# Eight k-tiles instead of six through seven block products in the gate and up projections of a decoder layer

## The chip, the cores and the metric

The kernel runs on one core of a Trainium2 chip. Its time is the device time of one launch in microseconds (us), as the median of three runs. The weights lie in HBM in float32, 461 MB are read from it in a launch, and the token block is short (256 tokens), so every weight is read once and used for two blocks of 128 tokens.

## The reference

One layer: half a SwiGLU, a mixer (dilated attention beside a gated spatial unit, merged by two sigmoid gates), half a SwiGLU again, and a final norm. The change is in the gate and up projections of the two SwiGLUs; the rest moves only because it shares buffers with them.

```python
def swiglu(x, w_gate, w_up, w_down):
    return (jax.nn.silu(x @ w_gate) * (x @ w_up)) @ w_down

x = x + 0.5 * swiglu(rmsnorm(x, ffn1_norm[i]), ffn1_w_gate[i], ffn1_w_up[i], ffn1_w_down[i])
x = x + hybrid_mixer(rmsnorm(x, mix_norm[i]), ...)
x = x + 0.5 * swiglu(rmsnorm(x, ffn2_norm[i]), ffn2_w_gate[i], ffn2_w_up[i], ffn2_w_down[i])
```

x is 256 x 2048, gate and up are 2048 x 5632, down is 5632 x 2048.

## The kernel before

**Products.** A float32 product is made of three TensorE matmuls on operands split in a high and a low part: high by high, high by low, low by high. The weight of a k-tile (128 rows, 512 columns) is split by two instructions: ACT copies it to `wh` (L356), and DVE subtracts `wh` from it to give `wl` (every DVE instruction has line L66, the wrapper that keeps count of DVE's work). `wh` and `wl` are rings of nine k-tiles. One matmul takes 128 tokens' activations as its weights and 512 columns of `wh` or `wl` as its moving operand, and all of them have line L363.

**Steps.** The program is one list of steps. A plain step ("n") is two k-tiles of one column group of 512: one load of 512 KB to a `raw` tile, one split on ACT and one on DVE, and 12 matmuls (two k-tiles, two token blocks, three matmuls). A loop over the steps writes out each step's products, then whatever has come due (evacuations, transpositions), then the splits of the steps ahead for which the ring has room, then additions that are put off until DVE has time. All engines work off what is theirs in that order.

**Seven products.** Two column groups that are computed together (gate and up of the same columns, or two column groups of down) and two token blocks form a 2 x 2 block product over some of the k-tiles, paired two by two. A "quad" does such a pair of k-tiles in seven block products (the Strassen and Winograd scheme) instead of eight, which are 21 matmuls and not 24. For that it needs seven forms of the four weight blocks, `p1` to `p7`: three are the blocks b11, b21 and b22 themselves; f is a sum of two blocks (mostly added by an accumulating DMA from the POOL queue while it is loaded), and t2, t1 and t4 are made by DVE additions. Each form is split like a raw tile and takes a quarter of a plain step per pair of k-tiles. Sums of the activations (`fx`, `fy`, `fh`) are needed too; they are made once. Between forms, partial results in PSUM are copied (ACT, L415, L417, L419) and added (DVE). The forms of a quad begin in the tail of the group before (`p1`, `p6`, `p7`) and end in the first half of its own (`p5`, `p4`, `p3`, `p2`).

**The two SwiGLUs.** There are 11 column groups of gate and up each. The first two of the first SwiGLU and the first of the second are done in other ways; the other 9 and 10 are quads over three pairs (six of the sixteen k-tiles), with ten plain steps for the rest. `silu` of gate is taken by ACT (L614) when gate's sum is complete, the product with up by DVE when up's is, then DVE transposes the result, a DMA writes it to DRAM and four read it back as the left operand of down. The tile `sg` in which this happens has two buffers (tag `tmp`). Loads of raw tiles (five buffers, and seven units more in the tiles C and E at the very start) are issued on the SP queue (L256), blocks of quads too (L298).

Of the kernel before, what the change touches and what calls it, by code (L numbers as in the profile page):

```python
# [44 lines left out]
RAWB = 5  # L45
MORE = 7
# [25 lines left out]
def layer(ctx: ExitStack, tc: tile.TileContext, a, out):  # L72
# [75 lines left out]
    def lay_out():  # L148
        i, count = 0, 0
        while i < len(gemms):  # L150
# [8 lines left out]
            if quad:  # L159
# [4 lines left out]
                quad["todo"] = ["t2", "t1", "t4"] if quad["adds"] else ["f", "t2", "t1", "t4"]  # L164
                for k, form in opening(count):
                    steps.insert(len(steps) - k, ("s", (quad, form)))
                for k, form in reversed(list(closing(len(order)))):
                    new.insert(k, ("s", (quad, form)))
# [8 lines left out]
        for kind, s in steps:  # L177
            width = 2 if kind == "n" else s[0]["nq"]
# [4 lines left out]
            if kind == "s":  # L183
                s[0].setdefault("at", {})[s[1]] = len(ends) - 1
# [56 lines left out]
    raws = {}  # L241

    def load_unit(i, first=0, end=2):
        if i not in raws and RAWB <= i < RAWB + MORE:
# [3 lines left out]
            raws[i] = raws["more"][:, 2 * o:2 * o + 2]  # L250
        if i not in raws:
            raws[i] = big.tile([P, 2, NC], F32, tag="raw", bufs=RAWB, name=f"raw{i}")
# [9 lines left out]
    def ffn_home(home):  # L262
        home["h"] = [big.tile([P, 16, S], F32R, tag=tag, name=f"h{tag}") for tag in "AB"]
        c, e = (big.tile([P, 4096], F32, tag=tag, name="quads") for tag in "CE")
        w = sb.tile([P, SGW], F32, tag="W", name="sum")
        b11, b21, b12, b22, t2 = (v.rearrange("p (q c) -> p q c", q=3)
                                  for v in (c[:, 0:SGW], c[:, SGW:2 * SGW], e[:, 0:SGW], e[:, SGW:2 * SGW], w))
        return b11, b21, b12, b22, t2, b11, e[:, 2 * SGW:2 * SGW + NC]
# [7 lines left out]
    def merge_home(home):  # L276
        l_ = sb.tile([P, 3, 2, NC], F32, tag="L", name="quads")
        w = sb.tile([P, 3, NC], F32, tag="W", name="part")
        t = sb.tile([P, 2, NC], F32, tag="tmp", bufs=2, name="sum")
# [12 lines left out]
    def load_block(quad, b):  # L292
# [6 lines left out]
        if b == 2 and quad["adds"]:  # L299
            POOL.dma_start(blocks_of(quad)[b], block(quad, 3), accum_op=OP.add)  # L300
# [46 lines left out]
    def split(i, k=None):  # L347
        kind, s = steps[i]
        if kind == "s":
            prepare_for(*s)  # L350
            s[0]["split"].add(s[1])
        r = raws[place[i]] if kind == "n" else form_of(*s)
# [5 lines left out]
        if kind == "s" and s[1] in FREES:  # L358
            at(now[0] + (1 if s[1] == "p5" else 2), lambda: load_block(next_of(s[0]), FREES[s[1]]))
# [952 lines left out]
```

## Time and profile before

| what | before |
|---|---|
| median of three runs | 1985.66 us (1984.95 to 1985.70) |
| the profiled execution | 1985.29 us, its span 1983.5 us |
| TensorE (PE) busy | 1971.1 us, 99% of the span, 9188 instructions |
| DVE busy | 1592.2 us, 80%, 1655 instructions |
| ACT busy | 1189.5 us, 60%, 1382 instructions |
| granted TensorE clock | 0.999 |
| DMA | 492.34 MB, mean 248 GB/s |

A row of a group of instructions reads: line, engine, operation, result<-operands, shape, count, then the busy time and the mean of one. In the table by windows each engine has its busy time in the stretch and, in brackets, how many of its instructions touch it; overlapping instructions of one engine count once. In a timeline the first number is the start and the second the duration, both in us. In a list of waits the numbers are the total, the count and the longest.

### The profile page before, as it was taken

What the parts mean: (1) busy time and instruction counts of PE and PEld (TensorE: products, weight loads), DVE (VectorE), ACT (ScalarE), POOL (GpSimd) and SP (SyncE); (2) the same over time, 40 slices, a digit from 0 to 9 for tenths busy, and PEclk for the clock granted to TensorE, in tenths of its full rate; (3) what the DMA queues carried; (4) which work ended last, traced back from release to release, by engine and by line L of the source; (5) the groups of instructions that cost most, each with busy time, mean ns of one, the idle gap of its engine ahead of it and who ended that gap; (6) DMA issues with size and microseconds to landing.
All of it is one profiled execution on the core that took longest, in us unless ns stands there. A gap on an engine that the chain in (4) does not pass through costs nothing.

```text
span 1983.5 us, 25183 instructions
## 1 busy us (share of the span) xinstructions
PE 1971.1 (99%) x9188; PEld 1723.6 (87%) x9188; DVE 1592.2 (80%) x1655; ACT 1189.5 (60%) x1382; POOL 51.7 (3%) x48
## 2 busy tenths in 40 slices
PE   9999999999999999999999999999999999999998
PEld 8888888888888888888888888878888888888887
DVE  6798888888897798766665777888898889888886
ACT  7566556665666676555454555576655566565664
POOL 0000100000000000000000000000000000000000
PEclk9999999999999999999999999999999999999999
DMA  9788778787777985888877667788888777878783
GB/s 323 256 279 271 237 238 266 247 254 245 247 242 226 289 294 186 254 275 255 264 238 249 210 204 231 237 260 267 255 252 260 234 249 247 252 250 254 244 265 123
DMA packets 264644, 492.34 MB, mean 248 GB/s; under 512 B 17484, under 2 KB 46024, under 8 KB 264392
## 3 DMA queue, kind: packets, MB, share of 16 engines
q1 hardware_dynamic: 253624, 469.49, 72.0%
q0 software_dynamic: 10576, 20.71, 6.0%
q8 instruction: 72, 1.18, 0.2%
q10 hardware_dynamic: 320, 0.53, 0.1%
q14 instruction: 52, 0.43, 0.1%
HBM read 461.01 MB, written 29.66 MB: 247 GB/s over the span
## 4 chain that ended last, share of the span: by engine, by line
PE 95%; DVE 2%; DMA 1%; issue 1%; ACT 0%; SPq 0%; POOLq 0%; POOL 0%; DVEq 0%; ACTq 0%
PE qd L363 71%; PE mm L363 22%; DVE wl L66 1%; DMA raw<-in_w_in_dram 0%; DMA quads<-in_w_in_dram 0%; DVE btx L66 0%; ACT wh L356 0%; PE sp L815 0%; PE warm L1180 0%; DMA xt<-bmx 0%; DVE xlo L66 0%; PE pv L990 0%; PE sc L953 0%; DVE x L66 0%; DVE quads L66 0%
## 5 line engine op out<-in xcount | busy, mean ns | idle before, releaser
L66 DVE TENSOR_TENSOR wl<-raw,wh 128x1024 fp32r<-128x1024 f32 (+1 forms) x636 | 695.7, 1112 | 184.5 <-ACT wh L356 182.8
L356 ACT ACTIVATE wh<-raw 128x1024 fp32r<-128x1024 f32 (+1 forms) x636 | 609.1, 966 | 365.8 <-PE qd L363 199.6
L363 PE MATMUL qd<-wh,xlo 128*128 128x512 f32 x1201 | 455.4, 379 | 1.0 <-DVE xlo L66 1.0
L363 PE MATMUL qd<-wh,xhi 128*128 128x512 f32 x1201 | 455.3, 379 | 0.0
L363 PE MATMUL qd<-wl,xhi 128*128 128x512 f32 x1201 | 455.2, 379 | 0.0
L356 ACT ACTIVATE wh<-quads 128x1536 fp32r<-128x1536 f32 (+2 forms) x226 | 250.9, 1117 | 271.1 <-PE qd L363 251.5
L66 DVE TENSOR_TENSOR wl<-quads,wh 128x1536 fp32r<-128x1536 f32 (+2 forms) x226 | 291.0, 1301 | 147.7 <-ACT wh L356 147.5
L363 PEld LDWEIGHTS qd<-wh,xlo 128*128 128x128 f32 x1201 | 227.0, 189 | 33.9 <-DVE xlo L66 1.8
L363 PEld LDWEIGHTS qd<-wh,xhi 128*128 128x128 f32 x1201 | 227.0, 189 | 32.4 <-issue 0.2
L363 PEld LDWEIGHTS qd<-wl,xhi 128*128 128x128 f32 x1201 | 227.0, 189 | 32.2
L363 PE MATMUL mm<-wh,xlo 128*128 128x512 f32 x608 | 230.6, 379 | 0.9 <-DVE xlo L66 0.8
L363 PE MATMUL mm<-wh,xhi 128*128 128x512 f32 x608 | 231.1, 380 | 0.1
L363 PE MATMUL mm<-wl,xhi 128*128 128x512 f32 x608 | 228.5, 379 | 0.0
L363 PE MATMUL qd<-wh,hA 128*128 128x512 f32 x564 | 213.8, 379 | 0.0
L363 PE MATMUL qd<-wl,hA 128*128 128x512 f32 x564 | 213.8, 379 | 0.0
L363 PE MATMUL qd<-wh,hB 128*128 128x512 f32 x564 | 213.8, 379 | 0.0
L356 ACT ACTIVATE wh<-sum 128x1024 fp32r<-128x1024 f32 (+2 forms) x85 | 101.4, 1196 | 86.7 <-PE qd L363 66.9
L66 DVE TENSOR_TENSOR wl<-sum,wh 128x1024 fp32r<-128x1024 f32 (+2 forms) x85 | 117.8, 1395 | 18.0 <-ACT wh L356 16.5
L363 PEld LDWEIGHTS mm<-wh,xlo 128*128 128x128 f32 x608 | 114.9, 189 | 17.8 <-DVE xlo L66 1.6
L363 PEld LDWEIGHTS mm<-wh,xhi 128*128 128x128 f32 x608 | 114.9, 189 | 16.2 <-ACT xhi L547 0.2
L363 PEld LDWEIGHTS mm<-wl,xhi 128*128 128x128 f32 x608 | 114.9, 189 | 16.1
L363 PE MATMUL qd<-wh,fx 128*128 128x512 f32 x352 | 119.2, 379 | 1.0 <-DVE part L66 1.0
(417 smaller groups left out, 2191.2 us busy)
## 6 DMA issues: line engine op xcount, KB each, us to landing
raw<-in_w_in_dram SPq DMA_DIRECT2D x168, 512.0 KB, 4.9
raw<-in_ffn_w_down_dram SPq DMA_DIRECT2D x120, 512.0 KB, 5.0
raw<-in_ffn_w_up_dram SPq DMA_DIRECT2D x112, 512.0 KB, 6.0
raw<-in_ffn_w_gate_dram SPq DMA_DIRECT2D x111, 512.0 KB, 4.2
quads<-in_ffn_w_gate_dram SPq DMA_DIRECT2D x38, 768.0 KB, 6.4
quads<-in_ffn_w_up_dram SPq DMA_DIRECT2D x38, 768.0 KB, 5.1
quads<-in_ffn_w_down_dram SPq DMA_DIRECT2D x32, 512.0 KB, 5.4
quads<-in_ffn_w_up_dram POOLq DMA_DIRECT2D x17, 768.0 KB, 10.6
```

Of the source, the lines that this page charges most:

```text
L66: return method(out, *args, **kwargs)
L356: ACT.activation(wh, r[:, first:end], AF.Copy)
L363: PE.matmul(g["ps"][t], act, in_turn(w), start=not g["begun"][t], stop=g["left"][t] == 0, skip_group_check=g["quad"] is not None)
```

## The change

Quads of gate and up take four pairs (eight k-tiles) instead of three, so such a group has eight plain steps instead of ten. A form of four pairs would take four of the nine slots of the ring at once; it is written as two pieces of two pairs, each with its own ACT and DVE split, and the additions that make it are still one instruction, over 2048 columns instead of 1536. The accumulating DMA of f is issued in two pieces as well.

The larger blocks need room. The tile W, one buffer of `tmp` and one raw tile are given up, and a tile V of 2688 columns takes W's place; t2 and a partial sum of the quads lie in V. With one `tmp` buffer a column group can't begin its `sg` while the one before still uses it, so `silu` moves from gate's end to up's end, and `holds` puts it off by a step as long as the tile is in use. In the mixer a second `tmp` (in V) and a fifth raw tile (`spare`) come back. The sums `fy` are made for two pairs instead of one, since eight k-tiles need them. The four blocks of a first quad are loaded spread over five steps and not at once.

```diff
-RAWB = 5
-MORE = 7
+RAWB = 4
+MORE = 8
...
+                chunks = [(0, nq)] if nq < 4 else [(q, q + 2) for q in range(0, nq, 2)]
                 for k, form in opening(count):
-                    steps.insert(len(steps) - k, ("s", (quad, form)))
+                    for c in chunks:
+                        steps.insert(len(steps) - k, ("s", (quad, form, *c)))
...
+    V = sb.tile([P, SGW + 9 * P], F32, name="V")
+    turns = dict(raw=0, tmp=0, both=False, held=False)
+
+    def five(i):
+        return not turns["held"] and any(hus[i][0]["w"] is w for w in in_mixer)
...
     def move_in(home):
         home["room"] = home["make"](home)
-        for b in (0, 2, 3, 1):
-            load_block(next(q for q in quads if q["home"] is home), b)
+        first = next(q for q in quads if q["home"] is home)
+        for b, wait in ((0, 0), (2, 1.5), (3, 3), (1, 5)):
+            at(now[0] + wait, lambda b=b: load_block(first, b))
...
         if b == 2 and quad["adds"]:
-            POOL.dma_start(blocks_of(quad)[b], block(quad, 3), accum_op=OP.add)
+            for q in range(0, quad["nq"], 2):
+                c = slice(q, min(q + 2, quad["nq"]))
+                POOL.dma_start(blocks_of(quad)[b][:, c], block(quad, 3)[:, c], accum_op=OP.add)
...
             elif n != 1 and c == CS[n] + 1:
-                sums_of(i + lag, xT, 2, 1, forms_tile(big, "k2", f"fy{n}", 1), src, f"y{n}", tag)
+                sums_of(i + lag, xT, 2, 2, store, src, f"y{n}", tag)
...
-                quad = dict(k0=4 * CS[n], nq=2 if late else 3, forms=xT, home=merge if late else home)
+                quad = dict(k0=4 * CS[n], nq=2 if late else 4, forms=xT, home=merge if late else home)
...
+                    if not early:
+                        if holds["sg"]:
+                            at(e + 1, lambda: me["again"](e + 1, banks))
+                            return
+                        me["go"]()
+                    sg = me["sg"]
+                    holds["sg"] = 2 if first == 0 or first == 1 and quads_here["nq"] == 3 else 1
...
-            while loaded < len(hus) and loaded < place[done] + RAWB:
+            while loaded < len(hus) and loaded < place[done] + (5 if five(loaded) else 4):
```

Three places show what moves. The first is DVE's queue in the first SwiGLU, from the splits of `p1` of one quad to the addition that makes t1 (`quads<-sum,quads`, later `quads<-V,quads`); `sum` or V holds t2 there, and `wl<-quads`, `wl<-sum` and `wl<-V` are splits of forms. Before:

```order
L66 TENSOR_TENSOR wl<-quads,wh 128x1536 x2
L66 TENSOR_TENSOR sum<-quads 128x1536
L66 TENSOR_TENSOR wl<-raw_2216,wh 128x1024
L66 TENSOR_TENSOR wl<-raw_2251,wh 128x512 x2
L66 TENSOR_TENSOR wl<-sum,wh 128x1536
L66 TENSOR_TENSOR wl<-raw_2266,wh 128x1024
L66 TENSOR_TENSOR quads<-sum,quads 128x1536
```

And in the changed kernel:

```order
L66 TENSOR_TENSOR wl<-quads,wh 128x1024 x2
L66 TENSOR_TENSOR wl<-quads,wh 128x512 x2
L66 TENSOR_TENSOR wl<-quads,wh 128x1024
L66 TENSOR_TENSOR V<-quads 128x2048
L66 TENSOR_TENSOR wl<-raw_2228,wh 128x1024
L66 TENSOR_TENSOR wl<-raw_2276,wh 128x1024
L66 TENSOR_TENSOR wl<-V,wh 128x1024 x2
L66 TENSOR_TENSOR wl<-raw_2314,wh 128x1024
L66 TENSOR_TENSOR quads<-V,quads 128x2048
```

`p2` of one quad and `p1` of the next stand together in both; they are two instructions of 1536 columns before and four pieces of 1024 now (one of them cut in two where the ring wraps around). The plain steps between the forms are the same here, and the additions are a third longer.

The second is ACT's queue at the same quads: where `silu` (L614, later L655) of one column group stands, with the copy of a partial sum ahead of it (L415 follows `p1`, L450 follows `p7`). Before:

```order
L356 ACTIVATE wh<-sum 128x1536
L356 ACTIVATE wh<-raw_2266 128x1024
L415 ACTIVATE qd_0_2379<-qd_3_2382 128x512
L614 ACTIVATE sg117.5_2371<-qd_0_2105,rstd_440 128x512
L614 ACTIVATE sg117.5_2371<-qd_1_2106,rstd_440 128x512
L356 ACTIVATE wh<-raw_2297 128x1024
```

And in the changed kernel:

```order
L387 ACTIVATE wh<-quads 128x1024 x2
L450 ACTIVATE qd_1_2408<-qd_3_2410 128x512
L655 ACTIVATE sg117.5_2540<-qd_0_2129,rstd_439 128x512
L655 ACTIVATE sg117.5_2540<-qd_1_2130,rstd_439 128x512
L387 ACTIVATE wh<-raw_2417 128x1024
L498 ACTIVATE fh109.5_2443<-fsh109.5_2523 128x4x256
L387 ACTIVATE wh<-V 128x1024 x2
```

The pair of `silu` instructions moves from behind `p1` to behind `p7`, about half a group later, and there are still two.

The third is DVE's queue at the entry to the second SwiGLU, where `xt_1` is the second quarter of the normalized and transposed activations, and `fsy` and `fy` are sums of it and their low parts. Before:

```order
L66 TENSOR_TENSOR fsy_9714<-xt_1_9617 128x128
L66 TENSOR_TENSOR fsy_9714<-xt_1_9617,fsy_9714 128x128
L66 TENSOR_TENSOR wl<-raw_9601,wh 128x1024
L66 TENSOR_TENSOR sum<-quads,sum 128x1024
L66 TENSOR_TENSOR xlo_9402<-xt_1_9617,xhi_9401 128x1024
L66 TENSOR_TENSOR fy_9737<-fsy_9714,fy_9737 128x512
```

And in the changed kernel:

```order
L66 TENSOR_TENSOR fsy_9735<-xt_1_9638 128x256
L66 TENSOR_TENSOR fsy_9735<-xt_1_9638,fsy_9735 128x256
L66 TENSOR_TENSOR wl<-raw_9645,wh 128x1024
L66 TENSOR_TENSOR V<-quads,V 128x1024
L66 TENSOR_TENSOR xlo_9423<-xt_1_9638,xhi_9422 128x1024
L66 TENSOR_TENSOR fy2spare<-fsy_9735,fy2k_9758 128x1024
```

Each of the first two rows stands twice in the queue. The order is the same; the sums and the low part are twice as wide.

More of the change, by code (lines that the diff above doesn't have):

```diff
@@ L249, in load_unit, with tmp @@
                 raws["more"] = big.tile([P, 8, NC], F32, tag="C" if i == RAWB else "E", name=f"more{i}")
-            raws[i] = raws["more"][:, 2 * o:2 * o + 2]
+            return raws["more"][:, 2 * o:2 * o + 2]
+        turns["raw"] = (turns["raw"] + 1) % 5 if five(i) else 0
+        if turns["raw"] == 4:
+            return big.tile([P, 2, NC], F32, tag="spare", name=f"raw{i}")
+        return big.tile([P, 2, NC], F32, tag="raw", bufs=RAWB, name=f"raw{i}")
+    def tmp(shape, name):
+        turns["tmp"] = 1 - turns["tmp"] if turns["both"] else 0
+        if not turns["tmp"]:
+            return sb.tile(shape, F32, tag="tmp", name=name)
+        n = 1
+        for k in shape[1:]:
+            n *= k
+        v = V[:, SGW:SGW + n]
+        names = "abcd"[:len(shape) - 1]
+        return v.rearrange(f"p ({' '.join(names)}) -> p {' '.join(names)}", **dict(zip(names, shape[1:])))
+    def load_unit(i, first=0, end=2):
         if i not in raws:
-            raws[i] = big.tile([P, 2, NC], F32, tag="raw", bufs=RAWB, name=f"raw{i}")
+            raws[i] = raw_room(i)
         g, u, j = hus[i]
@@ L263, in ffn_home @@
         home["h"] = [big.tile([P, 16, S], F32R, tag=tag, name=f"h{tag}") for tag in "AB"]
[L264 to L268, printed above, removed]
+        c, e = (big.tile([P, 2, 4, NC], F32, tag=tag, name="quads") for tag in "CE")
+        t2 = V[:, 0:4 * NC].rearrange("p (q c) -> p q c", q=4)
+        return c[:, 0], c[:, 1], e[:, 0], e[:, 1], t2, c[:, 0], V[:, 4 * NC:5 * NC]
     def gate_home(home):
@@ L422, in read, with sums_of @@
                 DVE.tensor_tensor(q12, x_, part, op=OP.add)
-        after_splits.append(read)
-        if form in ("p1", "p7", "p5"):
-            (second if form == "p5" else first)["begun"][form == "p7"] = True
+        if q1 == quad["nq"]:
+            after_splits.append(read)
+            if form in ("p1", "p7", "p5"):
+                (second if form == "p5" else first)["begun"][form == "p7"] = True
         close(g, i)
-    def sums_of(i, keep, q0, nq, store, v, name, tag="gate", slack=1):
+    def sums_of(i, keep, q0, nq, store, v, name, tag="gate", slack=1, then=None):
         got = {}
@@ L587, in layer @@
     sides = [0]
+    holds = dict(sg=0)
     homes = []
@@ L840, in post @@
         def post(e, banks):
[L841 removed]
+            q = tmp([P, NT, NSLOT, HD], f"{key}{gi}")
             one = 2 * NSLOT * P
```

95 lines of the change are left out of this document (58 added, 37 removed).

## The prediction

> **What bounds the kernel now.** I read the page's head first, then the chain of waits in order of time, PE's own list of waits, and windows laid on single gate and up groups.
>
> ```profile
> span 1983.5 us, 25183 instructions
> PE 1971.1 (99%) x9188; PEld 1723.6 (87%) x9188; DVE 1592.2 (80%) x1655; ACT 1189.5 (60%) x1382; POOL 51.7 (3%) x48
> ...
> DVE  6798888888897798766665777888898889888886
> ```
> ```profile
> 96.55 543.91 PE qd L363 x2520
> ...
> 1327.49 642.74 PE qd L363 x2976
> ```
>
> The two long pieces of the chain are the two SwiGLUs from their first quads on: for 544 and 643 us the chain never leaves PE. A busy PE can still be slow, but here the pieces give its pace: 543.91/2520 and 642.74/2976 are both 0.216 us a matmul, and that is what one costs when it is removed.
>
> PE's waits, from its own list:
>
> ```profile
> PE qd L363 <- DVE part L66: 1.0, 1, 1.0
> PE qd L363 <- DVE xlo L66: 1.0, 2, 0.8
> PE warm L1180 <- PEq L1295: 0.8, 1, 0.8
> PE mm L363 <- DVE xlo L66: 0.8, 1, 0.8
> PE qd L363 <- DVE wl L66: 0.6, 1, 0.6
> ```
>
> They are 4.2 us in all. So PE sets the end, by the number of its matmuls, and a change that removes matmuls is worth their time as long as everything that feeds PE keeps up. The feeder that is nearest to not doing so is DVE. From the table by windows (PE, PEld, DVE, ACT, POOL, clock, DMA), where the first six are gate and up groups of 39.5 us:
>
> ```profile
> 99.00:138.50 39.50, 39.50 (x185) 34.59 (x184) 37.59 (x43) 25.60 (x28) 1.30 (x1) 1.00 0.86 280
> ...
> 257.00:296.50 39.50, 39.50 (x185) 34.59 (x184) 31.46 (x28) 23.63 (x27) 1.29 (x1) 1.00 0.74 231
> 296.50:336.00 39.50, 39.50 (x185) 34.59 (x184) 34.83 (x34) 25.31 (x27) 1.28 (x1) 1.00 0.80 252
> ...
> 1369.80:1409.30 39.50, 39.50 (x185) 34.53 (x184) 33.82 (x32) 25.42 (x27) 1.28 (x1) 1.00 0.79 246
> 1409.30:1448.80 39.50, 39.50 (x185) 34.59 (x185) 35.88 (x35) 24.75 (x26) 0.26 (x1) 1.00 0.83 263
> ...
> 1646.30:1685.80 39.50, 39.50 (x185) 34.59 (x184) 35.69 (x34) 24.79 (x28) 1.22 (x1) 1.00 0.84 259
> ```
> ```profile
> 1305.00:1330.00 25.00, 22.44 (x101) 18.53 (x101) 24.96 (x31) 19.51 (x30) 0.00 (x0) 1.00 0.76 235
> ...
> 745.00:775.00 30.00, 30.00 (x141) 26.27 (x140) 29.71 (x36) 21.97 (x30) 0.00 (x0) 1.00 0.48 150
> ```
>
> A group needs 31.5 to 37.6 us of DVE in 39.5. The last two rows show what a full DVE does: at the entry to the second SwiGLU it is busy for 24.96 of 25 us and PE loses 2.56 us; in the mixer it is busy for 29.71 of 30 us and PE loses nothing. Saturation alone does not decide; what counts is whether the ring's nine k-tiles cover the lateness.
>
> **The matmuls removed.** Nine groups of the first SwiGLU and ten of the second go from three pairs to four, and each pair saves one block product, 3 matmuls: 19 x 3 = 57, at 0.216 us 12.3 us. A group falls from 39.5 us (183 matmuls) to 180 x 0.216 = 38.9 us.
>
> **What DVE gets in return.** Starts that follow each other in DVE's timeline give what an instruction takes from the queue:
>
> ```profile
> 318.68 1.22 DVE L66 TENSOR_TENSOR wl<-raw,wh 128x1024 fp32r<-128x1024 f32 x1
> 319.82 1.75 DVE L66 TENSOR_TENSOR quads<-sum,quads 128x1536 f32<-128x1536 f32 x1
> 321.49 1.22 DVE L66 TENSOR_TENSOR wl<-raw,wh 128x1024 fp32r<-128x1024 f32 x1
> 322.62 0.68 DVE L66 TENSOR_TENSOR wl<-quads,wh 128x512 fp32r<-128x512 f32 x1
> ```
>
> 1.14 us for 1024 columns and 1.67 for 1536, so 0.535 more for each 512, and 2.21 for 2048 (an estimate from these two). Each instruction starts some 0.08 us before the one ahead has ended. Per group: seven forms as two pieces, 7 x (2 x 1.14 - 1.67) = +4.3; two plain steps fewer, -2.3; three additions of 2048 columns and not 1536, +1.6. That is +3.6 us of DVE in a group that is 0.6 us shorter. 34.83 becomes 38.4 of 38.9. Of the 19 groups, ten hold 33.8 to 37.6 us now and stay under 38.9 but for three: 37.59 + 3.6 is over by 2.3, 35.88 by 0.6, 35.69 by 0.4, together 3.3 us. The other nine, of which 257.00 is one, end near 35 and have air. Bounds for what this costs PE: nothing (745 to 775 us, full for 30 us without a stall) and, at the price of the entry, 2.56 us for each of ten groups, 26 us. A bound below nothing has no reason, since no work leaves DVE. I take half of the 3.3, 1.6 us, because the lateness of one group is made up in a lighter one and the ring hides some, while those that go over stay late for many steps.
>
> [...]
>
> **The entry to the second SwiGLU.** PE waits there for DVE's chain, and `fy` is in it.
>
> ```profile
> 1300.90 0.38 DVE L66 TENSOR_TENSOR fsx<-xt 128x256 f32<-128x256 f32 x1
> ...
> 1302.33 1.22 DVE L66 TENSOR_TENSOR wl<-quads,wh 128x1024 fp32r<-128x1024 f32 x1
> ...
> 1319.55 0.28 DVE L66 TENSOR_TENSOR fsy<-xt 128x128 f32<-128x128 f32 x1
> ...
> 1320.47 1.22 DVE L66 TENSOR_TENSOR wl<-raw,wh 128x1024 fp32r<-128x1024 f32 x1
> ...
> 1323.88 0.68 DVE L66 TENSOR_TENSOR fy<-fsy,fy 128x512 fp32r<-128x512 f32 x1
> 1324.48 1.22 DVE L66 TENSOR_TENSOR wl<-quads,wh 128x1024 fp32r<-128x1024 f32 x1
> ...
> 1326.75 0.68 DVE L66 TENSOR_TENSOR part<-part,qd 128x512 f32<-128x512 f32 x1
> ```
>
> Sums of two pairs (`fsx`) take 1.43 us, those of one (`fsy`) 0.92; the low part `fy` takes 0.60 and would take 1.14. That is 1.05 us more ahead of `part`, for which PE waits 1.0 us already, so it comes through whole: between 0 (if another wait covers it) and 1.05, I take 1.05. At the entry to the first SwiGLU the same sums fall into a stretch where DVE is six to seven tenths busy (the first two slices of the page's DVE line).
>
> **What lies beside other work.** ACT has 25 of 39.5 us: the form pieces and `silu` fit. `silu` is two instructions as before; at up's end they stand ahead of one raw split, and gate's banks are next wanted by the quad after the next. `holds` puts off only two column groups, by two steps and one, in the first SwiGLU, where nothing asks for them before down. Between `p6` and `p7` one plain step is left of two, 12 x 0.216 = 2.6 us, and in it ACT must copy PE's result:
>
> ```profile
> L417 ACT ACTIVATE quads<-qd 128x512 f32<-128x512 f32 x31 | 18.0, 579 | 0.0
> ...
> L356 ACT ACTIVATE wh<-raw 128x1024 fp32r<-128x1024 f32 x506 | 531.9, 1054 | 347.1 <-PE qd L363 192.2 <-PE mm L363 119.5 <-DMA raw<-in_w_in_dram 12.0
> ```
>
> One split ahead of it and the copy are 1.63 us. If that cover went, PE would lose up to 1.6 us in each of 19 groups; the step is there in all.
>
> POOL issues two accumulating DMAs of 512 KB for one of 768 KB, and behind them on its queue stands nothing until the next quad. Raw loads have four tiles for five, so a load is issued one plain step later:
>
> ```profile
> raw<-in_ffn_w_up_dram SPq DMA_DIRECT2D x112, 512.0 KB, 6.0
> ...
> quads<-in_ffn_w_up_dram POOLq DMA_DIRECT2D x17, 768.0 KB, 10.6
> quads<-in_ffn_w_down_dram POOLq DMA_DIRECT2D x8, 512.0 KB, 7.9
> ```
>
> Two in sequence are 16 us in a group of 39. For raw tiles: four plain steps without forms are 10.4 us; landing 6.0, ACT 1.05 and DVE 1.2 make 8.3, and in a group with forms the four steps stretch to some 19 us. In the mixer the fifth tile is back.
>
> **The sum.** The profiled execution took 1985.29 us, 0.37 less than the median, and its span lies 1.8 us inside it; neither offset moves, so the sum can stand on the median: 1985.66 - 12.3 + 1.6 + 1.05 = 1976.0 us.
>
> **The rivals.**
>
> 1. The full gain. The ring hides all of DVE's excess and the entry's extra second falls beside another wait: 1985.66 - 12.3 = 1973.4. For it: 745 to 775 us, and only 3.3 us of excess in 750 us. Against it: PE's list has DVE in nearly every line.
>
> 2. Late loads eat most of it. For it: ACT already waits for raw tiles where steps are plain and unbroken.
>
> ```profile
> ACT wh L356 <- DMA raw<-in_w_in_dram: 12.9, 10, 2.2
> ...
> ACT wh L356 <- DMA raw<-in_ffn_w_gate_dram: 6.7, 6, 4.1
> ```
>
> A tile fewer makes a load 2.6 us later. Over the six of the last row that is 15.6 us more of ACT's waiting; the ring has kept all of the 6.7 us from PE so far, and if it keeps two thirds of the new ones too, 5 us are left: 1976.0 + 5 = 1981. Against it: none of these waits reaches PE's list.
>
> 3. DVE becomes the bound. If instructions hide nothing of each other, a group's DVE time is what the durations sum to: 34.83 plus 34 x 0.08 is 37.6; added are 7 x (2.44 - 1.76) - 2.44 + 3 x 0.54 = 3.9; the group takes 41.5 us instead of 39.5. Ten groups lose 2.0, nine still gain 0.6: 1985.66 + 20 - 5.4 = 2000. It decides from the point at which such a group needs over 39.5 us, that is 1.1 us more than my 38.4. Idle time of DVE that can't be used, because the ring is full and DVE waits for ACT and ACT for PE, does the same; it is 4.7 us a group now (39.5 - 34.83), and must fall under 0.5.
>
> That the change doesn't do what it says I give no chance: the matmuls are counted from the loops.
>
> **How the numbers follow.** The forecast 50%, the full gain 27%, late loads 14%, DVE as the bound 9%. A difference of 0.2%, 4 us, is what this kernel's runs can tell from none, so faster is under 1981.7. The forecast and the full gain are faster, late loads are so in half: 84%; the other half of them and a little of the third are the same, 9%; slower 7%. The range reaches from 1972.5, which is the full gain and a microsecond of the entry's old waits, to 1982.5, where late loads end; beyond it lies DVE as the bound.
>
> **What would show it.** Right: 57 fewer matmuls; chain pieces still unbroken in both SwiGLUs at 0.216 us a matmul; windows of 38.9 us on gate and up groups with DVE at 35 to 39 us in them; PE's waits some 7 us, with `part` at the entry near 2. Wrong: waits of PE for `wl` or of ACT for `raw` that repeat once a group (late DVE, late loads), a wait of PE for L448 between `p6` and `p7`, or of ACT's L655 for the one `tmp` tile. The forecast falls if groups last 39.5 us or more.

## The result, and the profile after

The changed kernel takes 2032.39 us (median of four runs, 2025.32 to 2033.30) against 1985.31 us before on the same chip: the ratio is 1.0232, with a 95% interval of 1.0208 to 1.0256. The forecast was 1976.0 us, in a range from 1972.5 to 1982.5: both the sign and the range were missed.

The head of the page and the chain of waits by engine and line, after:

```profile
span 2031.6 us, 25234 instructions
PE 1981.2 (98%) x9131; PEld 1719.4 (85%) x9131; DVE 1660.8 (82%) x1745; ACT 1231.9 (61%) x1472; POOL 76.8 (4%) x69
...
PE 62%; DVE 8%; DMA 6%; issue 5%; ACT 1%; POOL 0%; SPq 0%; DVEq 0%; POOLq 0%; ACTq 0%
PE qd L394 43%; PE mm L394 18%; DVE wl L66 5%; DMA quads<-in_ffn_w_up_dram 3%; DMA raw<-in_w_in_dram 1%; ACT wh L387 1%; DMA quads<-in_w_in_dram 1%; DVE V L66 1%; DMA xt<-bmx 1%; DMA bmh529.0_10447<-bth529.0_10444 0%; DVE quads L66 0%; ACT xt L611 0%; POOL quads L329 0%; DVE xlo L66 0%; DVE btx L66 0%
```

PE has the 57 matmuls fewer (9131 for 9188), and yet it is busy 10 us longer, and the chain now leaves PE for DVE, for DMAs and for time at which nothing is waited for. PE's own list of waits, after:

```profile
PE qd L394 <- DVE wl L66: 27.2, 22, 5.5
PE mm L394 <- DVE wl L66: 7.8, 4, 3.6
```

Before, the first of these rows was 0.6 us in a single wait. PE stands still for `wl` 26 times, for 35 us. The windows (columns as before) show what such waits look like from three sides:

```profile
347.30:389.00 41.70, 39.85 (x181) 33.73 (x180) 39.37 (x39) 30.49 (x36) 2.75 (x3) 1.00 0.80 247
534.70:573.60 38.90, 38.90 (x182) 34.06 (x181) 35.87 (x35) 23.89 (x26) 2.82 (x3) 1.00 0.84 268
...
465.00:475.00 10.00, 4.72 (x22) 3.78 (x20) 3.23 (x2) 2.30 (x3) 0.00 (x0) 0.93 0.66 185
475.00:480.00 5.00, 4.75 (x11) 3.85 (x12) 5.00 (x7) 2.72 (x4) 0.00 (x0) 0.50 0.63 191
```

The second row is a group as forecast: 38.9 us, PE never idle. The first is one that is not: 41.7 us, with DVE idle for 2.3 us of them. The last two rows lie where a down part of the first SwiGLU ends and gate and up of column group 8 begin. There PE stands for half of ten microseconds, and DVE and ACT are idle for two thirds and three quarters of them, so nobody is saturated, somebody waits for data. And after the wait the granted clock is 0.50: PE "busy" for 4.75 us does 11 matmuls. Five stalls are followed by such a stretch, 58 matmuls in all, which take some 13 us more than they would at full pace. Together with some 0.26 us by which the matmuls at the two ends of most stops are longer, they are why PE is busy for longer with fewer matmuls.

To see where the time came from I took, for each quad, the time from its first `p5` matmul to that of the next quad, less 0.216 us for each matmul between, and subtracted the same of before. This gives the loss by place, in us:

| place | changed kernel |
|---|---|
| first SwiGLU's entry (start to the first quad's `p5`) | 7.9 |
| gate and up quads that follow a down quad (three of the four lose: at 470, 1580 and 1805 us) | 21.0 |
| other groups of the two SwiGLUs | 21.0 |
| entry to the mixer (PE stands between 719 and 725 us) | 8.6 |
| entry to the second SwiGLU | 1.3 |
| matmuls removed, 57 x 0.216 | -12.3 |
| sum | 47.5 |

The spans differ by 48.1 us. The gain of the products is there; four late feeds take it away. Each shows in the trace.

**The first SwiGLU's entry.** The timeline of ACT and DVE:

```profile
72.52 1.06 ACT L387 ACTIVATE wh<-raw 128x1024 fp32r<-128x1024 f32 x1 [2.82 <-DMA raw<-in_ffn_w_gate_dram]
80.54 2.28 DVE L66 TENSOR_TENSOR V<-quads 128x2048 f32<-128x2048 f32 x1
83.96 2.32 DVE L66 TENSOR_TENSOR wl<-raw,wh 128x1024 fp32r<-128x1024 f32 x2
```

ACT, and DVE behind it, wait for a raw tile; from then on DVE has no pause, and the splits of the last row, for which PE stands 2.96 us, are behind `t2` of the first quad (the row at 80.54). ACT waits for a raw tile here before the change too, 4.1 us at the longest, and PE does not stand; so the raw tile alone is not the cause.

**The quads behind a down quad.** The timeline at the first of the three that lose, in the first SwiGLU (POOL, then DVE and PE):

```profile
453.64 1.22 POOL L329 DMA_DIRECT2D quads<-in_ffn_w_up_dram  x1 [31.61 <-DVE hB L66]
462.18 1.21 POOL L329 DMA_DIRECT2D quads<-in_ffn_w_up_dram  x1 [7.32 <-issue]
...
471.77 2.29 DVE L66 TENSOR_TENSOR V<-quads 128x2048 f32<-128x2048 f32 x1 [7.04 <-DMA quads<-in_ffn_w_up_dram]
473.98 2.35 DVE L66 TENSOR_TENSOR wl<-raw,wh 128x1024 fp32r<-128x1024 f32 x2
...
475.25 0.79 PE L394 MATMUL qd<-wl,hA 128*128 128x512 f32 x1 [5.53 <-DVE wl L66]
```

POOL issues the first accumulating DMA of 512 KB at 453.64 and the second 8.5 us later, and in between the profile names nothing that it waits for ("issue"; of the 17 such pairs, 6.3 to 10.4 us apart, nine have the name of some DVE instruction there). The landings tell more than these names: in all 17 pairs the second is issued 0.26 to 0.34 us after the first has landed. The two never overlap. `t2` (`V<-quads`) needs the whole accumulated block, DVE takes its queue in order, and so two splits of raw tiles that were ready (ACT had ended their `wh` at 465.42 and 467.36 us) stand behind it for some 7 us and start at 473.98, and PE stands 5.5 us behind them.

**The other groups.** From ACT's list of waits:

```profile
ACT wh L387 <- DVE V L66: 39.3, 18, 6.8
...
ACT sg117.5_2540 L655 <- DVE fsh109.5_2523 L66: 5.2, 1, 5.2
...
ACT sg200.5_4079 L655 <- DVE fsh192.5_4062 L66: 4.8, 1, 4.8
```

There are six waits of the second kind, 29.0 us in all: `silu` wants the one transposition tile, in which DVE has not yet read the last column group's values for the sums `fsh`. `holds` does not prevent it, since it is released when the sums are written into the program, and DVE reaches them some 5 us later.

**Entry to the mixer.**

```profile
708.62 6.06 SPq L325 DMA_DIRECT2D quads<-in_w_in_dram  x1
...
720.21 1.22 DVE L66 TENSOR_TENSOR quads<-quads 128x1024 f32<-128x1024 f32 x1 [4.92 <-DMA quads<-in_w_in_dram]
```

With the four blocks spread over five steps the third to be loaded, b22 (the load above), lands at 720.18 us; DVE, which adds it to b12, has waited 4.92 us for it, and PE stands for 3.55 and 1.67 us.

### The profile page after: what moved, and what is told of

It is laid out like the page before. It is cut to its first block, busy times and chain, and to the rows that moved or that the text cites. A ratio compares the mean times of both kernels' runs of the same rounds, so it can differ in the third digit from the quotient of the medians.

```text
span 2031.6 us, 25234 instructions
## 1 busy us (share of the span) xinstructions
PE 1981.2 (98%) x9131; PEld 1719.4 (85%) x9131; DVE 1660.8 (82%) x1745; ACT 1231.9 (61%) x1472; POOL 76.8 (4%) x69
## 4 chain that ended last, share of the span: by engine, by line
PE 62%; DVE 8%; DMA 6%; issue 5%; ACT 1%; POOL 0%; SPq 0%; DVEq 0%; POOLq 0%; ACTq 0%
PE qd L394 43%; PE mm L394 18%; DVE wl L66 5%; DMA quads<-in_ffn_w_up_dram 3%; DMA raw<-in_w_in_dram 1%; ACT wh L387 1%; DMA quads<-in_w_in_dram 1%; DVE V L66 1%; DMA xt<-bmx 1%; DMA bmh529.0_10447<-bth529.0_10444 0%; DVE quads L66 0%; ACT xt L611 0%; POOL quads L329 0%; DVE xlo L66 0%; DVE btx L66 0%
## 5 line engine op out<-in xcount | busy, mean ns | idle before, releaser
L66 DVE TENSOR_TENSOR wl<-raw,wh 128x1024 fp32r<-128x1024 f32 (+1 forms) x593 | 647.0, 1110 | 205.1 <-ACT wh L387 202.7
L387 ACT ACTIVATE wh<-raw 128x1024 fp32r<-128x1024 f32 (+1 forms) x593 | 567.5, 966 | 362.2 <-PE qd L394 187.8
L387 ACT ACTIVATE wh<-quads 128x1024 fp32r<-128x1024 f32 (+2 forms) x315 | 308.3, 987 | 229.0 <-PE qd L394 206.5
L394 PE MATMUL qd<-wl,xhi 128*128 128x512 f32 x1106 | 420.9, 381 | 12.3 <-DVE wl L66 12.3
L394 PE MATMUL qd<-wh,xhi 128*128 128x512 f32 x1106 | 419.9, 380 | 1.9 <-ACT wh L387 1.9
L394 PE MATMUL qd<-wh,xlo 128*128 128x512 f32 x1106 | 419.3, 379 | 0.6 <-DVE xlo L66 0.6
L66 DVE TENSOR_TENSOR wl<-quads,wh 128x1024 fp32r<-128x1024 f32 (+2 forms) x315 | 349.7, 1136 | 76.6 <-ACT wh L387 74.8
L387 ACT ACTIVATE wh<-V 128x1024 fp32r<-128x1024 f32 (+2 forms) x128 | 124.6, 995 | 93.0 <-PE qd L394 46.2
L66 DVE TENSOR_TENSOR wl<-V,wh 128x1024 fp32r<-128x1024 f32 (+2 forms) x128 | 143.0, 1141 | 16.1 <-ACT wh L387 15.2
L394 PEld LDWEIGHTS qd<-wl,hA 128*128 128x128 f32 x564 | 108.3, 192 | 30.2 <-DVE wl L66 14.4
```

The source lines that it names most:

```text
L66: return method(out, *args, **kwargs)
L387: ACT.activation(wh, r[:, first:end], AF.Copy)
L394: PE.matmul(g["ps"][t], act, in_turn(w), start=not g["begun"][t], stop=g["left"][t] == 0, skip_group_check=g["quad"] is not None)
```

## The experiments

All edits are to the changed kernel unless another is named. The theory was that late feeds (these places) and not DVE's amount of work cost the time; the rival was that DVE is the bound. The table by place for each run is at the end of this section. Groups are counted from 0 in each SwiGLU. The runs were not all made on one chip; beside them the kernel before took 1983.8 to 1984.2 us, and 1985.3 beside the changed kernel, so 1 to 2 us of a difference between two runs can be the chip's.

**Three pairs again, all buffers kept.**

```diff
-                quad = dict(k0=4 * CS[n], nq=2 if late else 4, forms=xT, home=merge if late else home)
+                quad = dict(k0=4 * CS[n], nq=2 if late else 3, forms=xT, home=merge if late else home)
```

> The changed kernel, but the quads of gate and up take three pairs again (one word); every change of buffers, silu at up's end, the loads spread over five steps and the pieces of two stay. Theory (late feeds: the second accumulating DMA starts only when the first is done, 21.0 us at the three eight-tile quads that follow down; the spread loads at the mixer's entry, 8.6; the first SwiGLU's entry, 8.0; ACT held at silu for the one transposition tile together with a full DVE, 22.2): pieces of 512 and 256 KB run side by side as they do for down, and DVE has air, so the 21.0 and most of the 22.2 go, the two entries and some of the silu waits stay, and the 12.3 us of products are not won: 1985.3 + 8.6 + 8.0 + about 6 = 2008 us (2000 to 2014). Rival (DVE is the bound, by four products' larger forms alone): buffers cost nothing, 1985 to 1990 us.

Measured: 1997.71 us, ratio to before 1.0071 (1.0056 to 1.0086). Both theories were off: all of the change but the fourth pair costs 14 us, not 0 to 5 and not 23. The trace puts 7.5 of its 10.9 us of span at the mixer's entry and 2.4 in groups 2 and 3; the quads behind down lose nothing, and there the pieces of 512 and 256 KB are issued back to back (of POOL's 50 issues 29 have idle time ahead of them, one for each of the 21 pairs and the 8 single ones). So the rest of the change hurts by itself at the mixer's entry, and elsewhere nearly only together with the fourth pair.

**The first blocks loaded at once.**

```diff
-        for b, wait in ((0, 0), (2, 1.5), (3, 3), (1, 5)):
+        for b, wait in ((0, 0), (2, 0), (3, 0), (1, 0)):
```

> The changed kernel, but the four blocks of a first quad are loaded at once, as before, in all three places. Theory (late feeds): the fourth block no longer comes 5 steps late at the mixer's entry, DVE's addition waits no 4.92 us, and PE's 3.72 + 2.05 us there with the slow matmuls behind them go: 8.6 us less, 2024 us; if the first SwiGLU's entry (8.0 us) hangs on the same spreading, 2016. Rival (DVE is the bound): 2032, no change.

Measured: 2024.64 us, 7.7 less than the changed kernel; the mixer's entry falls from 8.6 to 1.4 us and the first SwiGLU's entry from 7.9 only to 6.9. The spreading is the mixer's cause, and not that of the first entry.

**More room for the POOL queue's descriptors.**

```diff
-    pad = big.tile([P, 96], F32, name="pad")
+    pad = big.tile([P, 64], F32, name="pad")
...
-    nc = _bacc.Bacc("TRN2", target_bir_lowering=False, num_devices=1, dynamic_dma_scratch_size=1024)
+    nc = _bacc.Bacc("TRN2", target_bir_lowering=False, num_devices=1, dynamic_dma_scratch_size=1152)
```

> The changed kernel with 1152 bytes a partition for the descriptors of the POOL queue's DMAs and not 1024 (a padding tile is shorter by as much, so no other tile moves). Theory (late feeds; the second accumulating piece waits for room in the descriptor ring): the two pieces of 512 KB are issued within about 1 us of each other as those of down are, the waits of DVE's t2 for the block (21.8 us) go, and the three eight-tile quads behind down lose 21.0 us less: 2011 us. Rival 1 (the queue takes one accumulating DMA at a time whatever the room): the second issue stays 6 to 10 us behind the first, 2032. Rival 2 (DVE is the bound): the pieces come earlier, the time stays within 5 us of 2032.

Measured: 2004.31 us (2002.12 to 2007.35), 28 us less. The same two issues in the timeline, and PE's first wait in the list:

```profile
447.10 2.47 POOL L329 DMA_DIRECT2D quads<-in_ffn_w_up_dram  x2 [31.26 <-DVE hB L66]
```
```profile
PE qd L394 <- DVE wl L66: 9.8, 15, 1.0
```

The two DMAs are issued back to back (one row, 2.47 us for both), the three quads behind down lose 0.2 us for 21.0, and of PE's 27.2 us 9.8 are left with nothing over 1.0. So 128 bytes a partition were worth more than half of the loss. Other groups, where the block was a little late too, give back 5.5 us. The first entry has 3.0 for 7.9, but that place takes no accumulating DMA, and the later runs with the same ring have 5.0 to 6.8 there, so part of it is scatter; without it the table gives the ring 26 us.

**`silu` put off by two steps more behind the sums.**

```diff
+                    def later():
+                        at(now[0] + 2, let_go)
...
-   sums_of(e + 10, st, 0, 2, lambda: [st["fs"][:, h, :, 0:2] for h in range(2)], src, f"h{e}", slack=3, then=let_go)
+   sums_of(e + 10, st, 0, 2, lambda: [st["fs"][:, h, :, 0:2] for h in range(2)], src, f"h{e}", slack=3, then=later)
```

(and the same for the sums of one pair).

> The changed kernel, but after a column group whose sums for down are taken from the transposition tile, silu of the next group is put off by two steps more, so that ACT reaches it when DVE has read the tile. Theory (late feeds): the six waits of ACT for the tile, 29 us in all, go, and with them that part of the stalls in the gate and up groups which follows on them, 6 to 15 of 22.2 us: 2017 to 2026 us. Rival (DVE is the bound, ACT waits only for what is late anyway): 2032, no change, ACT's waits merely move to other rows.

Measured: 2034.89 us, 2.5 more and not 6 to 15 less. The six waits of `silu` for `fsh` are gone as intended, but two others stand in ACT's list, and one in PE's:

```profile
ACT fh109.5_2443 L498 <- DVE fsh109.5_2523 L66: 3.7, 1, 3.7
...
ACT sg57.0_1437 L655 <- DVE hB L66: 3.3, 1, 3.3
```
```profile
PE qd L394 <- DVE hB L66: 5.2, 2, 2.6
```

The first is ACT's copy of the sums to their high part, `fh`. It needs the same sums from DVE, and there are five such waits of 3.4 to 3.7 us. The weight splits behind it come late as before (DVE idles for 2.09 us in group 6), and the five groups with these waits, 6 and 10 of both SwiGLUs and 2 of the second, lose 2.3 to 2.7 us each, against 2.5 to 2.9 in the changed kernel. So the rival was right that ACT's waits would move to other rows. The hole does not hang on `silu` alone: it comes when ACT has to stand for DVE's late sums in front of the next weight split. The other rows are new losses: the column group that is put off is late, and at the start of two down parts PE now waits for `hB`, its low part, 5 us each time by the table.

**The mixer's blocks at once, with the larger ring.** From here on the runs build on the run with the larger ring.

```diff
-            at(now[0] + wait, lambda b=b: load_block(first, b))
+            at(now[0] + (0 if home is gates else wait), lambda b=b: load_block(first, b))
```

> The kernel with the larger descriptor ring (2004.3 us), and of the three places where blocks are loaded spread over five steps, the mixer's entry alone loads its four at once again. Theory (late feeds): the 90.5 us from the last down quad to the mixer's second quad become the 82.7 to 84 us of before, so 6.5 to 7.8 us less in all: 1996.5 to 1998. Rival (the entry is late for raw loads, one tile fewer, and the spreading only showed it): 2002 to 2006.

Measured: 1997.86 us, 6.4 less; the entry to the mixer loses 1.8 us instead of 7.8. As the theory said.

**The sums from another tile** (larger ring, blocks spread). DVE makes as many sums of the same width, but of the token block `x`: the quads of down then compute with sums of the wrong numbers, and nothing else is left out.

```diff
+                        elsewhere = x[:, 0, 0:2 * NC].rearrange("p (i m b) -> p m i b", i=4, b=32)
...
-   sums_of(e + 10, st, 0, 2, lambda: [st["fs"][:, h, :, 0:2] for h in range(2)], src, f"h{e}", slack=3, then=let_go)
+   sums_of(e + 10, st, 0, 2, lambda: [st["fs"][:, h, :, 0:2] for h in range(2)], elsewhere, f"h{e}", slack=3, then=let_go)
```

> The kernel with the larger descriptor ring, but the sums of activations for down (fsh) are taken from the token block x and not from the transposition tile: as many instructions of the same width on DVE, and only the wait of silu for them is gone (down's quads then compute with wrong sums; nothing else is left out). Theory (the single transposition tile: ACT stands 4.8 us before silu, then DVE has nothing to split and later too much): the six waits of 4.2 to 4.8 us go, and so do the stalls in groups 2, 6 and 10 of both SwiGLUs, 15.5 us: 1989 us (1987 to 1994). Rival (DVE is full in those groups by its own work): the same instructions, the same stalls, 2002 to 2006.

Measured: 1991.27 us, 13.0 less than with the larger ring alone. This is the run that separates the two theories. The same group 6, first with the larger ring alone and then without the wait:

```profile
341.10:382.50 41.40, 39.91 (x182) 33.77 (x181) 39.07 (x38) 30.49 (x36) 2.90 (x3) 1.00 0.79 243
```
```profile
340.70:379.70 39.00, 39.00 (x181) 33.92 (x180) 38.95 (x39) 28.43 (x33) 2.96 (x3) 1.00 0.84 260
```

DVE does the same work, 39.07 and 38.95 us. With the wait the group takes 41.4 us and without it 39.0. In the second row DVE is busy for all of the group and PE loses nothing. What cost the time was the hole that the wait tears into a DVE with no air, and not the work. (ACT still waits 2.69 us for the sums at `fh`, but `silu` and a raw split stand in front of that wait, so that DVE has work meanwhile.) The hole can be seen in the run with the larger ring:

```profile
341.34 0.42 DVE L66 TENSOR_TENSOR fsh109.5_2523<-sg102.5_2254,fsh109.5_2523 128x256 f32<-128x256 f32 x1
344.04 1.23 DVE L66 TENSOR_TENSOR wl<-raw,wh 128x1024 fp32r<-128x1024 f32 x1 [2.28 <-ACT wh L387]
...
341.79 1.27 ACT L655 ACTIVATE sg117.5_2540<-qd,rstd 128x512 f32<-128x512 f32 x2 [4.81 <-DVE fsh109.5_2523 L66]
```

ACT stands 4.81 us in front of `silu` until DVE has made the last sum; the raw split queued behind `silu` comes late, and so DVE, just done, has nothing to do for 2.28 us.

**The sums sooner** (larger ring, mixer's blocks at once).

```diff
-   sums_of(e + 10, st, 0, 2, lambda: [st["fs"][:, h, :, 0:2] for h in range(2)], src, f"h{e}", slack=3, then=let_go)
+   sums_of(e + 10, st, 0, 2, lambda: [st["fs"][:, h, :, 0:2] for h in range(2)], src, f"h{e}", slack=1, then=let_go)
```

> The kernel with the larger descriptor ring and the mixer's blocks at once, and the sums of activations for down are taken when they are ready and not put off by up to three steps, so DVE has read the transposition tile some 4 us sooner. Nothing is left out. Theory (the single transposition tile): the most of the 15.5 us in groups 2, 6 and 10 go: 1997 - 12 = 1985 us (1981 to 1990). Rival (DVE is full by its own work): the sums, 1.7 us, then stand ahead of weight splits and delay these instead: 1995 to 2000.

Measured: 1997.32 us, no change against 1997.86. The stalls of groups 6 and 10 moved a group ahead, to 5 and 9 (1.5 to 1.9 us each), as PE's list shows by a new first row:

```profile
PE qd L394 <- DVE V L66: 7.1, 7, 1.6
```

PE waits at `p5` for the subtraction of `part` (`V`), in front of which the sums and their low part now stand. The rival named this: the sums are in the way of other work of DVE's.

**The sums by POOL** (larger ring, mixer's blocks at once).

```diff
-            DVE.tensor_tensor(s1, a1, b1, op=OP.subtract)
+            on.tensor_tensor(s1, a1, b1, op=OP.subtract)
...
-   sums_of(e + 10, st, 0, 2, lambda: [st["fs"][:, h, :, 0:2] for h in range(2)], src, f"h{e}", slack=3, then=let_go)
+   sums_of(e + 10, st, 0, 2, lambda: [st["fs"][:, h, :, 0:2] for h in range(2)], src, f"h{e}", slack=1, then=let_go, on=POOL)
```

(all four subtractions, and both calls).

> The kernel with the larger descriptor ring and the mixer's blocks at once (1997.9 us), and the sums of activations for down are taken when they are ready, by POOL and not by DVE; nothing is left out. POOL is 4% busy. Theory (the single transposition tile, released late because DVE reads it in its own order): the tile comes free without DVE, and DVE's queue loses 1.7 us per group that has such sums, so the stalls in groups 2, 6 and 10 go as in the run without the wait, 13 to 16 us: 1984 us (1981 to 1988). Rival 1 (POOL's sums take longer than DVE's 1.7 us by so much that silu waits as long): the stalls stay, 1996 to 2000. Rival 2 (an accumulating DMA stands behind the sums on POOL's queue and comes late): the stalls move to the forms that wait for f, 1990 to 2000.

Measured: 2000.36 us, 2.5 more than before the edit and 16 more than expected. `silu` waits no longer in groups 5 and 9, but look at DVE while POOL is at work, in the timeline of POOL and of DVE:

```profile
325.05 2.36 POOL L471 TENSOR_TENSOR fsh109.5_2459<-sg102.5_2254 128x256 f32<-128x256 f32 x1 [14.07 <-DMA sg102.5_2254<-bmh109.5_2297]
327.49 1.60 POOL L472 TENSOR_TENSOR fsh109.5_2459<-sg102.5_2254,fsh109.5_2459 128x256 f32<-128x256 f32 x1
...
326.73 3.43 DVE L66 TENSOR_TENSOR wl<-raw,wh 128x1024 fp32r<-128x1024 f32 x2
330.09 3.42 DVE L66 TENSOR_TENSOR wl<-V,wh 128x1024 fp32r<-128x1024 f32 x2
```

Two splits take 3.43 us instead of the 2.35 in the row at 473.98 above. Over the whole run, the 23 splits of 1024 columns that fall within POOL's sums take 1.60 us on average, and those that meet none of them 1.22. Four sums on POOL, 7.4 us long, cost DVE 2.2 us and save it 1.7. Why DVE's splits take longer while POOL adds, no run shows. None of the three readings written down ahead named this. In group 2 of the first SwiGLU, though, the first rival took place: there ACT waits 4.9 us at `silu` and 5.2 at `fh` for POOL's sums, and that group alone loses 6.3 us.

**Three pairs in the first quad of each SwiGLU** (with POOL's sums).

```diff
-   quad = dict(k0=4 * CS[n], nq=2 if late else 4, forms=xT, home=merge if late else home)
+   quad = dict(k0=4 * CS[n], nq=2 if late else 3 if f == 2 - n // 2 else 4, forms=xT,
+               home=merge if late else home)
```

> The kernel of the run before this one (sums by POOL), and the first quad of each SwiGLU's blocks takes three pairs and not four, all others four: 6 matmuls more, 1.3 us. Theory: the first SwiGLU's entry (2.6 to 3.1 us of stall at 80 us and up to 3 us of slow matmuls behind it) and that of the second are late because four blocks of 1 MB are loaded beside the raw tiles, and because the additions for f and t2 are 2.28 us each; with three pairs, 5 us come back at the first entry and 0 to 3 at the second: 1978 us (1975 to 1982), which is faster than before. Rival (the entries are late for four raw tiles in place of five): 1.3 us slower than the run before this one, 1985.

Measured: 1991.47 us, 8.9 less than with POOL's sums alone, though six matmuls came back; the 1978 expected had taken POOL's sums for a gain. The loss at the first entry falls from 5.0 to 0.8 us, and in the groups right behind the two first quads from 6.3 to 3.3 and from 1.4 to 0.1. So that entry's lateness came with the fourth pair (blocks of 1 MB and additions of 2.28 us beside the raw tiles) and not from the fourth raw tile alone; which of the two, blocks or additions, no run separates.

**t1 twice** (on top of that).

```diff
-        DVE.tensor_tensor(out, x, y, op=op)
+        for _ in range(2 if what == "t1" and quad["nq"] == 4 else 1):
+            DVE.tensor_tensor(out, x, y, op=op)
```

> The kernel with the first quads at three pairs, and DVE makes t1 twice in each quad of four pairs (the second time the same numbers to the same place): 2.2 us more of DVE in each of 17 groups, nothing else. Theory (DVE is not the bound as long as its late moments fall into the ring; it has 0 to 4 us of idle time a group): groups that now need 34.6 to 36.4 us of DVE still fit, the six that need about 39 of 39 lose 2 us each and some of that to the group after: 10 to 16 us slower than without it, 1990 us. Rival (DVE is the bound in all groups): 17 x 2.2 = 37 us slower, 2015. Third reading (DVE has room): no change, 1978.

Measured: 2018.11 us, 26.6 more for 17 x 2.2 = 37 us of DVE. Group 5 without and with:

```profile
301.10:342.10 41.00, 39.36 (x181) 33.69 (x180) 38.51 (x35) 28.10 (x33) 9.89 (x6) 1.00 0.80 255
```
```profile
302.90:346.30 43.40, 39.62 (x182) 33.74 (x181) 42.38 (x37) 28.08 (x33) 9.27 (x7) 1.00 0.79 247
```

Seven tenths of it come through, more than the theory's 10 to 16 us. That is an average of groups that differ: groups 4 and 8 of the two SwiGLUs, where DVE had 34.5 to 35.4 us of work in 38.9 before the edit, lose 0.0 to 0.2 us more, and the six that lose most, where it had over 38, 2.3 to 2.6 us each. So this work was free where DVE had air and cost all of its length where it had none; most groups of this kernel have little or none, the more so with POOL's sums.

**Two tiles in turn** (larger ring, mixer's blocks at once, three pairs in the first quads, no sums on POOL).

```diff
+   me["sg"] = sg = (sb.tile([P, NT, NC], F32, tag="gate", bufs=2, name=f"sg{e}") if f % 2
+                    else tmp([P, NT, NC], f"sg{e}"))
...
+            for out, p_, q_ in ((b1, a1, b1), (a1, a1, a0), (a0, a0, b1), (b0, b0, a0)):
+                DVE.tensor_tensor(out, p_, q_, op=OP.subtract)
```

(the second part makes the four sums in the group's own tile, so that no other tile is needed for them; `holds` puts nothing off any more).

> The kernel with the larger descriptor ring, the mixer's blocks at once and three pairs in the first quad of each SwiGLU (without POOL's sums), in which column groups take turns in two tiles: even ones in the transposition tile, odd ones in one of the two tiles called gate. So that these are free, DVE takes the sums for down in place, in the group's own tile. Nothing is left out and nothing is put off. Theory (silu's wait for the one tile is what stalls groups 2, 6 and 10, and neither the place of the sums in DVE's order nor their 1.7 us): the stalls go as in the run without the wait, and 1997.9 - 14 - 6 = 1978 us (1974 to 1984), faster than before. Rival (what counts is that DVE has two low parts, the sums and the product with up to make around up's end, and is full there): the stalls stay or move to the form p5, as they did with POOL's sums, 1988 to 1996.

Measured: 1982.26 us (eleven runs, 1979.70 to 1984.85) against 1983.90 of before: ratio 0.9992 (0.9983 to 1.0001). The 50 us are back. Group 6, and the longest rows of PE's waits:

```profile
336.70:375.60 38.90, 38.90 (x181) 33.92 (x180) 38.87 (x39) 28.69 (x33) 2.89 (x3) 1.00 0.83 257
```
```profile
PE qd L394 <- DVE xlo L66: 2.1, 3, 1.1
PE qd L394 <- DVE V L66: 1.9, 2, 1.6
```

DVE is busy for 38.87 of 38.90 us and PE is not held up. All groups of the two SwiGLUs together lose 1.8 us.

**`fy` later** (on top of that).

```diff
-   sums_of(i + lag, xT, 2, 2, store, src, f"y{n}", tag)
+   sums_of(i + lag + (4 if n else 0), xT, 2, 2, store, src, f"y{n}", tag)
```

> The kernel in which column groups take turns in two tiles (1982.3 us), and at the entry to the second SwiGLU the sums fy (four instructions, 1.7 us) and their low part (1.2 us) are made four steps later, behind part, the two additions to x and one split; nothing is left out. Theory (the step of the prediction on this entry: DVE's chain ahead of part is what PE waits for, and fy is in it): PE's waits for xlo and V there, 3.7 us now, fall to about 1, and the time by 2 to 3 us: 1980 us. Rival (the entry is late for other reasons, raw loads or the blocks, and the 2.9 us of DVE are then missing further on): 1982 to 1984.

Measured: 1981.74 us (1979.17 to 1984.91), ratio 0.9989 (0.9980 to 0.9998); against the run without it no difference that can be told. In the trace the entry to the second SwiGLU loses 2.0 us for 3.9, and PE's waits for `xlo` and `V` there fall from 3.7 to 0.4 us, with a new one of 1.4 for `qd`; a stall of 1.6 us in group 2 of the first SwiGLU, where nothing was edited, hides it in the total.

The loss by place in every run's profiled execution, in us against before, as in the table above:

| run | first entry | behind down | groups | mixer's entry | second entry | matmuls | sum |
|---|---|---|---|---|---|---|---|
| changed kernel | 7.9 | 21.0 | 21.0 | 8.6 | 1.3 | -12.3 | 47.5 |
| three pairs, buffers kept | 0.4 | 0.0 | 2.4 | 7.5 | 0.2 | 0 | 10.5 |
| all blocks at once | 6.9 | 17.5 | 19.1 | 1.4 | 2.8 | -12.3 | 35.4 |
| larger ring | 3.0 | 0.2 | 15.5 | 7.8 | 2.4 | -12.3 | 16.6 |
| `silu` later | 5.4 | 19.8 | 25.3 | 8.0 | 2.5 | -12.3 | 48.7 |
| ring, mixer at once | 5.2 | 0.0 | 15.5 | 1.8 | 3.1 | -12.3 | 13.3 |
| ring, sums from another tile | 5.3 | 1.1 | 1.2 | 10.7 | 4.9 | -12.3 | 10.9 |
| ring, mixer, sums sooner | 6.8 | 0.5 | 14.7 | 1.4 | 1.8 | -12.3 | 12.9 |
| ring, mixer, POOL's sums | 5.0 | 0.6 | 17.5 | 1.4 | 2.1 | -12.3 | 14.3 |
| the same, first quads three pairs | 0.8 | 0.0 | 12.3 | 2.0 | 1.9 | -11.0 | 6.0 |
| the same, t1 twice | 0.7 | 5.6 | 35.4 | 1.2 | 2.8 | -11.0 | 34.7 |
| two tiles in turn | 0.7 | 0.2 | 1.8 | 1.4 | 3.9 | -11.0 | -3.0 |
| the same, `fy` later | 1.0 | 0.3 | 3.5 | 1.3 | 2.0 | -11.0 | -2.9 |

Single executions of one kernel lie up to 10 us apart (1987.10 to 1996.65 us with the sums from another tile), so a difference of 2 us between two rows of a column that the edit does not touch means nothing (the second entry and the mixer's of the run with sums from another tile, say). The column "groups" has all groups that do not follow a down quad; "behind down" has all four quads that do.

## Why the prediction was wrong, step by step

*The matmuls removed, -12.3 us.* Right: 57 fewer, and a group that is not held up takes 38.8 to 38.9 us, as forecast.

*What DVE gets, 3.6 us a group.* Right: DVE's busy time grew by 68.6 us, which is 3.6 for each of 19 groups. Its price, 1.6 us, was right in size where nothing else disturbs: with two tiles in turn all groups lose 1.8. There is luck in that, since the group that was to be furthest over (at 99.00) loses nothing there, because the quad in front of it has three pairs in that version, and the 1.8 us are spread over other groups. And the price was written down as if it stood alone. With DVE busy for all or nearly all of a group, a hole of 2.28 us came through to PE (group 6 took 41.4 us for 39.0), and so did 2.2 us of work that were added (2.3 to 2.6 us more in the six groups that lost most). The prediction looked for work above the capacity, and not for waits that cut into it. The third rival, DVE as the bound at 2000 us, took place in that form only: the kernel stays under it as long as nobody interrupts DVE.

*"POOL issues two accumulating DMAs of 512 KB for one of 768 KB, and behind them on its queue stands nothing until the next quad."* This step failed, and it is the largest miss: put at nothing, it cost 28 us by the run with the larger ring, 21 of them at three quads behind down. "Two in sequence are 16 us in a group of 39" was even near what happened (18 us from the first issue to the end of DVE's wait), but nothing was set against it: `t2` needs the block right after `p1`, and behind down the block is issued late. The question to ask was when the block is needed, and not how long the queue is free; and who stands behind the one who waits for it, as the two ready splits did behind `t2` until 473.98 us.

*"The form pieces and `silu` fit"*, at nothing. This failed for 13.0 us (the run with sums from another tile). ACT had the time, but `silu` was moved behind a release that is decided while the program is written and not when DVE is done, and it stands in front of a raw split. The list of what would show the forecast wrong names exactly this wait ("ACT's L655 for the one `tmp` tile"), and no price was put to it.

*Blocks spread over five steps, and raw tiles,* at nothing. The spreading cost 6.4 us at the mixer's entry (7.7 when undone in all three places). The first quads of four pairs cost some 10 us (8.9 us less, with six matmuls more): by the table 4.2 at the first SwiGLU's entry and most of the rest in the groups right behind. Of the second rival, late loads at 1981, the mechanism appeared at the entries and not in the groups: at the mixer's with a block and not with raw tiles, and at the first SwiGLU's only together with the fourth pair.

*The entry to the second SwiGLU, +1.05 us.* Not shown either way: the place loses 1.3 us in the changed kernel, and moving `fy` took 1.9 away, but it lost only 0.2 us in the run with three pairs, whose `fy` is as wide, and up to 4.9 in another. That 1.3 is near 1.05 counts for nothing beside this scatter.

*What the sum had no term for:* a long stall cost more than its length here. After its five longest stalls, of 2.96 us and more, the changed kernel's next 8 to 14 matmuls take 0.43 us each, some 13 us more in all than at 0.216.

The parts measured one after the other, 28.1, 6.4, 13.0 and 8.9 us, would lead from 2032.4 to 1976.0 (that this is the forecast's number is chance); the runs with all of them mended took 1982.3 and 1981.7. The difference of 6 us is not accounted for part by part. Of what is left against the full 11.0 us of that version, its profile puts 0.7 at the first entry, 1.4 at the mixer's, 3.9 at the second and 2.0 in groups. So the change, with its feeds mended, ends where before was, at best 0.1% ahead (0.9980 to 0.9998); no version here is ahead of the kernel before by the 0.2% that the prediction took for the least that can be told.

## What to carry to other kernels

When an edit cuts a transfer in two or gives up a buffer, ask for each when its result is first needed and what stands behind the waiting instruction in its engine's queue; spare time on the queue or on the engine answered neither here (POOL was 4% busy, and three quads whose second piece came late lost 21.0 us). A DVE that was busy for 38.95 us of a group of 39.00 cost nothing by that, but a supplier's wait that left it idle for 2.28 us made the same group 2.4 us longer, so price the waits that an edit adds together with the busy share, and not one by one. A wait that was named as what would refute the forecast should get a price before the forecast is made.

## What was not expected of the hardware

*With 128 bytes more for descriptors, accumulating DMAs overlapped.* With 1024 bytes a partition for POOL's descriptors, two of 512 KB for one quad are issued 6.3 to 10.4 us apart, and 512 and 256 KB (for the down quads of three pairs) back to back, 2.14 to 2.17 us for both; with 1152 bytes two of 512 KB go back to back too, in 2.47 us. That the ring's room is what POOL waited for is inferred from this one change of size and from the landings: in all 17 pairs the second was issued 0.26 to 0.34 us after the first had landed. The trace gives the wait no semaphore of its own.

*Half pace after a stall.* In the changed kernel's profile the five longest stalls of PE, of 2.96, 5.53, 3.55, 3.05 and 4.64 us, were each followed by 8 to 14 matmuls at 0.43 us. The granted clock was 0.50 for 6.83 us at four of them (from 473.69 to 480.52 us, say) and for 3.41 us at the one of 3.05 (from 1583.02). Behind its stalls of 1.04, 1.58 and 1.80 us the matmuls went on at 0.216 us, and so they did behind the one of 1.04 us before. Where the limit lies, and whether it is one of length, was not shown.

*POOL's sums slow DVE*: two splits took 3.43 us instead of 2.35 while POOL was at its sums, as shown above.
